# Every operand of the split float32r products at a multiple of 256 bytes in SBUF

## The chip, the core and the metric

The kernel runs on one core of one Trainium2 chip. Its time is the time on the device of one execution, in microseconds (us). The core has a matrix engine (TensorE, PE in the profile; its weight loads are shown apart, as PEld), a vector engine (DVE), an activation engine (ACT), GpSimd (POOL), and queues that start DMA transfers (SP). SBUF is the memory on the chip, 128 partitions wide; an address below is the place of a tile inside each partition, in bytes.

## What is computed

A trunk of two layers on 512 tokens of 1,024 features, all in float32:

```python
for l in range(DEPTH):                       # 2
    h = rms_norm(x, ffn1_norm[l])
    x = x + 0.5 * swiglu_ffn(h, ffn1_w_gate[l], ffn1_w_up[l], ffn1_w_down[l])
    h = rms_norm(x, mix_norm[l])
    (a_q, ..., c_g) = jnp.split(h @ w_in[l], SPLIT_IDX, axis=-1)
    o_a, o_b, o_c = hgrn2_mixer(...), gated_deltanet_mixer(...), retention_mixer(...)
    x = x + jnp.concatenate([o_a, o_b, o_c], -1) @ w_out[l]
    h = rms_norm(x, ffn2_norm[l])
    x = x + 0.5 * swiglu_ffn(h, ffn2_w_gate[l], ffn2_w_up[l], ffn2_w_down[l])
return rms_norm(x, final_norm)
```

`swiglu_ffn` is `(silu(h @ wg) * (h @ wu)) @ wd` with 2,816 hidden features. The three mixers are recurrences over the tokens, worked out in chunks.

## The kernel before, in words

**Split products.** A float32 product of the dense layers is made of float32r products, which run in one pass. Both factors are split: a weight `w` into `hi` (w rounded to float32r, by ACT) and `lo` (w less hi, by DVE or POOL), the activations likewise into `xh`/`xl` (line 379, `split_x`), `ah`/`al` (the gated activations) or `mh`/`ml` (the mixers' outputs). The sum takes three products, hi·hi, hi·lo and lo·hi, for each 128 rows of the contraction; `mm3` (line 202) issues them, line 208 in the profile. A product has a stationary operand of 128 x 128 (in the two-part FFN and the "fm" parts this is a block of the weights) and a moving operand of up to 512 columns (the activations). In the "tm" parts of the mixers it is the other way round: activations stationary, 256 columns of weights moving.

**Weights.** A unit is 128 columns of weights for up to 1,024 rows, 128 x 8 x 128 numbers. `load` (line 183) fetches two units with one DMA into `raw`; `split` (line 194) makes `hi` and `lo` of one unit, in pools of W_BUFS = 4 slots each. One kind of unit, with 264 columns, needs 1,056 numbers, and so every slot is 4,224 bytes long.

**The FFN** (`ffn`) goes through its hidden features in three groups of 8, 8 and 6 units. In a group, `pg` (gate) and `pu` (up) sums alternate, 24 products each; then come the `pd` (down) sums over the group's units, 24 or 18 products each. The last FFN's last `pd` sums run by halves of the tokens, 256 columns at a time (`end`).

**The mixers** (`mix`, `interleave`). The dense products (`ps_fm`, `ps_tm`, `ps_out`, line 251) fill the time in which the chains of the three mixers wait; the order is written out when the program is built, from a rough count of time, and the scheduler that builds the program then moves instructions of an engine within it.

**Where the operands lie.** Pools follow one another in SBUF in the order in which they are opened (from line 1416). In the built program the constants end such that all `xh`/`xl` tiles begin 32 bytes past a multiple of 256. The `hi` and `lo` slots begin alternately 32 and 160 bytes past one, since 4,224 is 16.5 times 256; as gate and up units alternate, every gate unit sits in a slot at 32 and every up unit in one at 160. The pool `m` of 50 tiles of 2,048 bytes, which holds `ah`, `al`, `mh`, `ml`, comes last; its tiles begin 96 bytes past a multiple of 256. The constant matrices `ident` and `tri`, used by transposes and by a few float32 products such as `ps_gr`, begin 128 bytes past one.

**A constant of the mixers.** `b_blocks` starts an inverse from 16 x 16 unit matrices: line 655 copies them from the constants (`eye16`, 256 columns of the constant table) to `blk_x` on POOL.

Of the kernel before, what the change touches and what calls it, by code (L numbers as in the profile page):

```python
# [45 lines left out]
# 2*pi in parts of 12 bits, so that products with integers below 2**12 are exact  # L46
# [12 lines left out]
def constants():  # L59
# [5 lines left out]
    # inside blocks of 32 tokens  # L65
# [6 lines left out]
    parts["eye16"] = np.broadcast_to(np.eye(16).reshape(1, 256), (P, 256))  # L72
# [23 lines left out]
W_BUFS = 4  # L96
STEP = 1600
# [7 lines left out]
# units of the mixers' weights whose lower parts Pool works out  # L105
POOL_LO = range(2, 70, 2)
GROUP = {"a": 0, "b0": 1, "b1": 2, "c": 3}
# the output projection takes the groups of heads in these parts
OUT_PARTS = (('b0', 'c'), ('b1',), ('a',))
PLAN = 't0 b0 a0 ai cq b1 ck bz0 cg a1 ag bz1'  # L110
# chains of each kind that run at once, and all that hold a PSUM bank
# [5 lines left out]
class Engine:  # L117
    """an engine whose instructions are timed roughly, for the order in which the chains' steps are put down."""
# [5 lines left out]
    def __getattr__(self, name):  # L124
        f = getattr(self.engine, name)

        def call(*args, **kw):
# [10 lines left out]
            # functions that need a table keep their order, so that tables change as seldom as planned  # L138
# [22 lines left out]
class Kern:  # L161
# [12 lines left out]
    def t2(self, name, dtype=F32):  # L174
        """512 numbers on each partition, from the pool that all such tiles share."""
        return self.m.tile([P, T], dtype, tag="m", name=name)
# [17 lines left out]
    def split(self, src, shape):  # L194
        hi = self.whi.tile(shape, F32R, tag="hi", name="hi")
        lo = self.wlo.tile(shape, F32R, tag="lo", name="lo")
        self.nc.scalar.copy(hi, src)
        self.count += 1
        (self.nc.gpsimd if self.count in POOL_LO else self.nc.vector).tensor_tensor(lo, src, hi.bitcast(F32), ALU.subtract)
        return hi, lo  # L200

# [9 lines left out]
    def dense_units(self, src, nk, narrow=0, begin=0):  # L211
        """weights in units of 128 columns, loaded 256 at a time but for the first few."""
# [8 lines left out]
    def stream_units(self, plan, w_out):  # L221
        """loads and splits of the weights of a plan and of the output projection, unit by unit."""
# [26 lines left out]
    def mmr(self, ps, a, b, start, stop):  # L249
        """a float32r product; counts the tensor engine's time."""  # L250
        self.nc.tensor.matmul(ps, a, b, start=start, stop=stop)  # L251
        self.spend(np.prod(b.shape[1:]) * 0.42)

    def mmf(self, ps, a, b, start=True, stop=True):
        """a float32 product; counts the tensor engine's time."""
# [13 lines left out]
    def dense_stream(self, plan):  # L269
        """(x*w) @ w_in, a matrix product at a time; each part goes to its callback, not yet scaled by rstd.  # L270
        "fm": 128 features on partitions; "tm": 128 tokens on partitions."""
        for kind, cols, done in plan:
# [16 lines left out]
            else:  # L289
                n = sum(w for _, w in cols)  # L290
                # two token blocks that share a bank are one accumulation group
# [28 lines left out]
        # the output projection but for its last part  # L320
# [17 lines left out]
    def out_rows(self, part):  # L338
        """row blocks of a part of the output projection; how many blocks of columns a unit of its weights has."""
        return [2 * GROUP[g] + i for g in part for i in range(2)], 4 // len(part)  # L340

    def out_part(self, ps, w, i, j, k, start, stop):
        """128 rows of the output projection's sum."""
# [5 lines left out]
    def room(self, n):  # L349
        """leaves n banks for the next dense products: parts that wait to be taken up are, if need be."""  # L350
# [8 lines left out]
    def prepare(self, d, w):  # L359
        """x[d] is final for this stage: its part of the mean square, and the split x*w."""  # L360
# [26 lines left out]
    def rsqrt(self, out, v, shape):  # L387
        """out = v ** -0.5 for a small positive tile: a guess from the exponent, then Newton steps."""
# [30 lines left out]
    def gated(self, pg, pu):  # L419
        """silu(gate) * up, split."""  # L420
# [17 lines left out]
    def ffn(self, wg, wu, wd, layer, norm, meanwhile=None, begun=None):  # L438
        nc = self.nc
        xs = list(self.xs)  # L440
        for gi, (f0, nf) in enumerate(GROUPS):
            act, queue = [], deque()
            gu, uu = self.gate_up(wg, wu, gi) if gi or not begun else begun
            # the first sums wait for the factors of the rows
# [31 lines left out]
    def end(self, units, act, nf):  # L476
        """the last sums and the final norm, by halves of the tokens: the first half leaves while the second is summed.
        x * weight goes to tokens on partitions, then come the row factors."""
# [23 lines left out]
    def to_rows(self, y, i, g):  # L502
        """half of the features of a half of the tokens, tokens on partitions."""
# [31 lines left out]
    def b_gates(self, l, ba):  # L535
        """beta, and the cumulative log decay of each 128 tokens, tokens on partitions."""
# [32 lines left out]
        # the same with heads on partitions, split: rows 0.. and 32.. add up to it  # L569
# [4 lines left out]
    def b_conv(self, l, ps, ch, kind):  # L574
        nc = self.nc
        raw = self.mb.tile([P, CONV_K - 1 + T], F32, tag="braw", name="braw", bufs=2)
# [13 lines left out]
    def b_start(self, l, heads):  # L590
        """silu and l2 norms (over the features, tokens on partitions) for a pair of heads."""
# [14 lines left out]
        # sums over the features, each on the partition of its token  # L606
# [15 lines left out]
    def to_tok(self, src):  # L622
        """blocks of 128 columns, each transposed."""
# [5 lines left out]
    def b_blocks(self, heads):  # L629
        """for a pair of heads the inverses of the diagonal blocks of 16, row by row with a block to a partition;  # L630
        32 x 32 transposes lead there and back."""
# [3 lines left out]
        # [(q b r), k, (head, chunk, b)] -> [(q, head, chunk, b), k, r]  # L635
# [15 lines left out]
        # row k of X: e_k - sum over r < k of N[k, r] X[r]; X as [m, k], twice in the end  # L651
# [3 lines left out]
        nc.gpsimd.tensor_copy(x1, self.c("eye16").rearrange("p (m k) -> p m k", k=16))  # L655
# [22 lines left out]
    def b_chain(self, l, h, q, k, v, k_tm, rq):  # L678
        """gated delta rule of one head in chunks of 128; yields where a result is waited for."""
# [21 lines left out]
        # decays: exp of differences of the cumulative log decay  # L701
# [16 lines left out]
        # attn^T and (N beta)^T  # L718
# [9 lines left out]
        # X = (I + N beta)^-1: blocks of 16 first, then by doubling: X <- X - X C X  # L728
# [5 lines left out]
        # blocks of 32: one to as many partitions  # L734
# [53 lines left out]
        # chunks in order; the products of one share a bank  # L788
# [32 lines left out]
    def open(self, group):  # L821
        """room for the outputs of a group of heads: 256 columns, tokens on partitions, two blocks to a tile."""
# [3 lines left out]
    def head_done(self, group):  # L826
        """the group goes on to norm and gate when its heads and its gate are there."""
# [4 lines left out]
    def out_group(self, group):  # L832
        """head norms and gates of 256 columns; then the same with features on partitions, split in two."""
# [27 lines left out]
    def a_chain(self, l, heads):  # L861
        """HGRN2 for a pair of heads: (z, q) each; yields where a result is waited for."""
# [17 lines left out]
        # log f over [1e-20, 1] within the range of Ln: the part below 2**-40 apart  # L880
        odd = lambda t: t.rearrange("p (n r) -> p n r", r=2)[:, :, 1]
        los = {}
        for h, (z, q) in heads.items():
# [3 lines left out]
            # odd tokens: q * f and k / f  # L887
# [14 lines left out]
    def a_head(self, l, h, b, q, k):  # L902
# [5 lines left out]
        # attention inside 64 tokens, level by level: the later half of each 2s tokens sees the earlier half;  # L908
        # up to 32 tokens in blocks of 32, one to as many partitions
# [5 lines left out]
        # q and k of odd tokens have the step to them within, so that both of a pair share the even one's decay  # L915
# [29 lines left out]
        # all levels up to 64 tokens share a bank  # L945
# [17 lines left out]
        # pairs of tokens  # L963
# [15 lines left out]
        # decays from the start and to the end of each 64  # L979
# [29 lines left out]
        # what the chunks before each 128 hold: rows of the second 64 pass the first one's total, columns alike  # L1009
# [33 lines left out]
    def rope_tables(self):  # L1043
        """cos and sin of positions * frequencies, tokens on partitions."""
# [468 lines left out]
```

## Time and profile before

| what | value |
|---|---|
| median of 3 runs (lowest to highest) | 2222.67 us (2220.6 to 2222.72) |
| span of the profiled execution | 2224.8 us |
| PE busy | 2190.6 us, 98% |
| PEld busy | 1838.3 us, 83% |
| DVE busy | 1143.8 us, 51% |
| ACT busy | 841.2 us, 38% |
| POOL busy | 497.2 us, 22% |
| DMA, share of 16 engines | 29.0% for the kernel's own queue |

The profiled execution is one more execution than the three runs; its span is what the profile gives for its time, and it is 2.1 us above their median. Matrix products overlap in the pipeline: a product's duration in the profile (about 0.39 us for 512 columns) holds its way through the array, and the pace is the step from one product's start to the next one's.

### The profile page before, as it was taken

Reading aid. Unit: us, or ns where it says so; the run is one execution under the profiler, and the core shown is the slowest. Engines: PE = TensorE matmul, PEld = TensorE weight load, DVE = VectorE, ACT = ScalarE, POOL = GpSimd, SP = SyncE. Lnnn points to the kernel's source line nnn. Section 1 sums busy time; section 2 is a strip of 40 time slices with the busy share of each in tenths; the row PEclk is TensorE's granted clock in tenths of the full one; section 3 lists DMA queues with packets and bytes.
Section 4 is the critical chain, followed back from the end, with each engine's and each line's share of the span. In section 5 each row is a group of like instructions: output and inputs, shape, how many; then the busy total and the mean of one; then the engine's idle time right before and its main releaser. Section 6 shows DMA issues by size and latency. Waiting matters only on the chain.

```text
span 2224.8 us, 31771 instructions
## 1 busy us (share of the span) xinstructions
PE 2190.6 (98%) x13079; PEld 1838.3 (83%) x13079; DVE 1143.8 (51%) x1980; ACT 841.2 (38%) x1319; POOL 497.2 (22%) x462
## 2 busy tenths in 40 slices
PE   9999999998999999999999999999999999999998
PEld 7888888887988788888888888888889888888888
DVE  5444335468487743433543343354766876333335
ACT  4322223555455422222332222244654544222225
POOL 2101012454333210101211010133633412101011
PEclk9999999999999999999999999999999999999999
DMA  5323234221113223232332323242211232323223
GB/s 153 127 76 114 76 104 138 71 76 40 58 58 105 94 96 95 76 114 76 95 112 97 95 95 95 81 130 75 77 51 37 77 105 80 110 84 106 86 94 124
DMA packets 197758, 203.21 MB, mean 91 GB/s; under 512 B 7627, under 2 KB 189293, under 8 KB 197613
## 3 DMA queue, kind: packets, MB, share of 16 engines
q1 hardware_dynamic: 197612, 201.18, 29.0%
q8 instruction: 103, 1.69, 0.3%
q14 instruction: 43, 0.34, 0.0%
HBM read 194.87 MB, written 6.29 MB: 90 GB/s over the span
## 4 chain that ended last, share of the span: by engine, by line
PE 87%; DVE 8%; ACT 2%; issue 1%; POOL 0%; DMA 0%; SPq 0%; DVEq 0%; ACTq 0%; POOLq 0%
PE pu L208 22%; PE pd L208 22%; PE pg L208 21%; PE ps_fm L251 8%; PE ps_tm L251 5%; PE ps_out L251 2%; DVE aw L144 1%; PE ps_scan L256 1%; DVE lo L144 1%; PE ps_ss L256 1%; DVE x L144 1%; DVE flo L144 1%; PE ps_ao L256 1%; DVE af L144 1%; ACT hi L144 1%
## 5 line engine op out<-in xcount | busy, mean ns | idle before, releaser
L144 ACT CAST hi<-raw 128x1024 fp32r<-128x1024 f32 (+2 forms) x369 | 377.6, 1024 | 1135.3 <-PE pd L208 325.9
L144 DVE TENSOR_TENSOR lo<-raw,hi 128x1024 fp32r<-128x1024 f32 (+2 forms) x325 | 390.0, 1200 | 79.7 <-ACT hi L144 61.9
L144 POOL TENSOR_TENSOR g<-g,rstd 128x512 f32<-128x512 f32 x88 | 149.7, 1701 | 1152.9 <-ACT g L141 1152.9
L208 PE MATMUL pd<-ah,lo 128*128 128x512 f32 (+1 forms) x752 | 284.8, 379 | 0.0
L208 PE MATMUL pd<-al,hi 128*128 128x512 f32 (+1 forms) x752 | 284.3, 379 | 0.0
L208 PE MATMUL pd<-ah,hi 128*128 128x512 f32 (+1 forms) x752 | 284.2, 378 | 0.0
L208 PE MATMUL pu<-xh,hi 128*128 128x512 f32 x704 | 279.0, 396 | 0.1
L208 PE MATMUL pu<-xh,lo 128*128 128x512 f32 x704 | 278.2, 395 | 0.0
L208 PE MATMUL pu<-xl,hi 128*128 128x512 f32 x704 | 277.8, 395 | 0.0
L208 PE MATMUL pg<-xl,hi 128*128 128x512 f32 x704 | 275.7, 392 | 0.6 <-DVE xl L144 0.6
L208 PE MATMUL pg<-xh,lo 128*128 128x512 f32 x704 | 275.4, 391 | 0.0
L208 PE MATMUL pg<-xh,hi 128*128 128x512 f32 x704 | 275.1, 391 | 0.1
L144 DVE TENSOR_TENSOR u<-pu,g 128x512 f32<-128x512 f32 x88 | 60.9, 692 | 292.6 <-PE pu L208 277.1
L144 DVE SCALAR_TENSOR_TENSOR x<-pd,x 128x512 f32<-128x512 f32 (+1 forms) x104 | 67.4, 649 | 239.5 <-PE pd L208 239.5
L144 DVE TENSOR_TENSOR g<-pg,rstd 128x512 f32<-128x512 f32 x88 | 60.8, 691 | 209.7 <-PE pg L208 209.2
L208 PEld LDWEIGHTS pd<-al,hi 128*128 128x128 f32 x752 | 141.2, 188 | 29.4
L208 PEld LDWEIGHTS pd<-ah,hi 128*128 128x128 f32 x752 | 141.1, 188 | 28.9
L208 PEld LDWEIGHTS pd<-ah,lo 128*128 128x128 f32 x752 | 141.2, 188 | 28.3
L208 PEld LDWEIGHTS pu<-xh,lo 128*128 128x128 f32 x704 | 132.6, 188 | 31.3
L208 PEld LDWEIGHTS pu<-xl,hi 128*128 128x128 f32 x704 | 132.9, 189 | 30.7
L208 PEld LDWEIGHTS pu<-xh,hi 128*128 128x128 f32 x704 | 132.6, 188 | 30.8 <-ACT hi L144 0.5
L208 PEld LDWEIGHTS pg<-xl,hi 128*128 128x128 f32 x704 | 132.4, 188 | 30.2 <-DVE xl L144 1.8
(331 smaller groups left out, 3791.4 us busy)
## 6 DMA issues: line engine op xcount, KB each, us to landing
raw<-in_ffn_w_gate_dram SPq DMA_DIRECT2D x43, 1024.0 KB, 5.3
raw<-in_ffn_w_up_dram SPq DMA_DIRECT2D x43, 1024.0 KB, 5.4
raw<-in_ffn_w_down_dram SPq DMA_DIRECT2D x32, 1024.0 KB, 5.0
raw<-in_w_in_dram SPq DMA_DIRECT2D x20, 1024.0 KB, 5.4
raw<-in_w_in_dram SPq DMA_DIRECT2D x32, 512.0 KB, 3.8
raw<-in_ffn_w_down_dram SPq DMA_DIRECT2D x20, 768.0 KB, 4.4
xd<-x SPq DMA_DIRECT2D x16, 256.0 KB, 2.2
raw<-in_w_out_dram SPq DMA_DIRECT2D x16, 256.0 KB, 2.7
```

The costliest lines, as they stand in the source:

```text
L144: return f(*args, **kw)
L208: self.nc.tensor.matmul(ps, a[:, k, :], b, start=n == 0, stop=n == 3 * nk - 1)
L251: self.nc.tensor.matmul(ps, a, b, start=start, stop=stop)
L256: self.nc.tensor.matmul(ps, a, b, start=start, stop=stop)
```

## The change

The operands' places are moved; what is multiplied by what stays. Four edits do it:

- a pool `pad` of 56 numbers (224 bytes) after the constants, so that the `xsp` pool begins at a multiple of 256 bytes;
- every weight slot is 1,088 numbers (4,352 bytes, 17 times 256) long, and the unit takes its first part (`unit`);
- the pools `m` and `mb` are opened before `tiny`, and the convolution's `braw` (2,060 bytes) gets a pool of its own at the end, so that nothing of an odd length lies ahead of `m`;
- `eye16` leaves the constant table, which makes room; `blk_x` is set by two memsets.

```diff
-    parts["eye16"] = np.broadcast_to(np.eye(16).reshape(1, 256), (P, 256))
...
+UNIT = 1088
+PAD = 56
...
     def split(self, src, shape):
-        hi = self.whi.tile(shape, F32R, tag="hi", name="hi")
-        lo = self.wlo.tile(shape, F32R, tag="lo", name="lo")
+        hi, lo = (self.unit(p, tag, shape) for p, tag in ((self.whi, "hi"), (self.wlo, "lo")))
...
+    def unit(self, pool, tag, shape):
+
+        t = pool.tile([P, UNIT], F32R, tag=tag, name=tag)
+        return t[:, 0:shape[1] * shape[2]].rearrange("p (k f) -> p k f", k=shape[1])
...
-        raw = self.mb.tile([P, CONV_K - 1 + T], F32, tag="braw", name="braw", bufs=2)
+        raw = self.conv.tile([P, CONV_K - 1 + T], F32, tag="braw", name="braw")
...
-        nc.gpsimd.tensor_copy(x1, self.c("eye16").rearrange("p (m k) -> p m k", k=16))
+        nc.gpsimd.memset(x1, 0.0)
+        nc.gpsimd.memset(x[:, 0:496:33], 1.0)
...
             self.const = pool("const", 1)
+            self.pad = pool("pad", 1)
+            self.pad.tile([P, PAD], F32, name="pad")
             self.xsp = pool("xsp", 1)
             self.wraw = pool("wraw", 2)
             self.whi = pool("whi", W_BUFS)
             self.wlo = pool("wlo", W_BUFS)
             self.tmp = pool("tmp", 1)
+            self.m = pool("m", M_BUFS)
+            self.mb = pool("mb", 1)
             self.tiny = pool("tiny", 2)
+            self.conv = pool("conv", 2)
             self.pa = pool("pa", 3, space=PSUM)
             self.pb = pool("pb", 5, space=PSUM)
-            self.mb = pool("mb", 1)
-            self.m = pool("m", M_BUFS)
```

In the built program of the change, all stationary operands of the split products and all their moving operands begin at a multiple of 256 bytes, but for 144 of the 192 products with 264 columns, whose rows of 1,056 bytes begin 32, 64 or 96 past one. `ident` and `tri` stay at 128. The order on PE in the FFNs is the same in both programs. In the mixers the new memsets make the scheduler move a few instructions by a place or some; two places show what that is like.

On POOL, at the start of the first pair's inverse (`blk_x` is the tile of the inverses, `ctmp` a tile of the rotations), before and now:

```order
L144 TENSOR_TENSOR lo<-raw,hi 128x1024
L144 COPY blk_x<-cst 128x16x16
L144 TENSOR_TENSOR ctmp<-craw,sin 128x256
L144 MEMSET aat 128x512
L144 TENSOR_TENSOR ae<-flo 128x128
```

```order
L147 TENSOR_TENSOR lo<-raw,hi 128x1024
L147 MEMSET blk_x 128x16x16
L147 MEMSET blk_x 128x16
L147 TENSOR_TENSOR ctmp<-craw,sin 128x256
L147 MEMSET aat 128x512
L147 TENSOR_TENSOR ae<-flo 128x128
```

One instruction has become two, at the same place.

On PE, in the first layer's mixers, where a chain's 32 small products (`ps_al`) stand among the dense products of a "fm" part (`ps_fm`), before and now:

```order
L251 MATMUL ps_fm<-xl_2477,hi 128x512
L251 MATMUL ps_fm<-xh_2476,lo 128x512
L251 MATMUL ps_fm<-xh_2509,hi 128x512
L256 MATMUL ps_al<-aq,ak 32x32 x32
L251 MATMUL ps_fm<-xl_2510,hi 128x512
```

```order
L258 MATMUL ps_fm<-xl_2484,hi 128x512
L258 MATMUL ps_fm<-xh_2483,lo 128x512
L263 MATMUL ps_al<-aq,ak 32x32 x32
L258 MATMUL ps_fm<-xh_2516,hi 128x512
L258 MATMUL ps_fm<-xl_2517,hi 128x512
```

The chain's products stand one dense product earlier; the products are the same ones.

## Rows read from the trace of the kernel before

**Rows 1.** The page, busy time, share of the span and instructions of PE.
```profile
PE 2190.6 (98%) x13079; PEld 1838.3 (83%) x13079; DVE 1143.8 (51%) x1980; ACT 841.2 (38%) x1319; POOL 497.2 (22%) x462
```
**Rows 2.** The page, chain that ended last, shares of the span by engine.
```profile
PE 87%; DVE 8%; ACT 2%; issue 1%; POOL 0%; DMA 0%; SPq 0%; DVEq 0%; ACTq 0%; POOLq 0%
```
**Rows 3.** The chain in order of time, first FFN: start us, us, engine, tile, products.
```profile
160.55 5.46 PE pg L208 x24
166.01 5.59 PE pu L208 x24
...
237.88 44.51 PE pd L208 x192
```
**Rows 4.** Groups of PE by form: tile<-operands, shapes, count, busy us, mean ns.
```profile
L208 PE MATMUL pu<-xh,hi 128*128 128x512 f32 x704 | 279.0, 396 | 0.1
...
L208 PE MATMUL pg<-xh,hi 128*128 128x512 f32 x704 | 275.1, 391 | 0.1
...
L208 PE MATMUL pd<-ah,hi 128*128 128x512 f32 x656 | 258.0, 393 | 0.0
...
L251 PE MATMUL ps_fm<-xh,hi 128*128 128x512 f32 x320 | 131.1, 410 | 1.7 <-issue 1.7
...
L251 PE MATMUL ps_tm<-hi,xh 128*128 128x256 f32 x448 | 129.5, 289 | 0.0
...
L251 PE MATMUL ps_out<-mh,hi 128*128 128x512 f32 x128 | 50.8, 402 | 1.0 <-DVE x L144 0.5 <-ACT mh L144 0.4
...
L208 PE MATMUL pd<-ah,hi 128*128 128x256 f32 x96 | 26.3, 277 | 0.0
```
**Rows 5.** Timeline of PE in an up unit: start us, duration us, product.
```profile
190.96 0.40 PE L208 MATMUL pu<-xl,hi 128*128 128x512 f32 x1
191.19 0.40 PE L208 MATMUL pu<-xh,lo 128*128 128x512 f32 x1
191.44 0.40 PE L208 MATMUL pu<-xh,hi 128*128 128x512 f32 x1
```
**Rows 6.** Timeline of PE from 446.61 us, first and last of six products.
```profile
446.61 0.63 PE L251 MATMUL ps_fm<-xl,hi 128*128 128x512 f32 x1
...
448.75 0.63 PE L251 MATMUL ps_fm<-xh,hi 128*128 128x512 f32 x1
```
**Rows 7.** The stretch around it: busy us (count) by engine, granted clock, DMA share, GB/s.
```profile
444.50:451.00 6.50, 6.50 (x21) 5.44 (x21) 2.27 (x13) 0.00 (x0) 0.72 (x1) 0.50 0.32 81
```
**Rows 8.** Timeline of PE at `ps_gr`: its first two products, then all eight.
```profile
403.86 0.41 PE L256 MATMUL ps_gr<-cst,g 128*36 128x128 f32 x2
...
403.86 1.06 PE L256 MATMUL ps_gr<-cst,g 128*36 128x128 f32 x8
```
**Rows 9.** Timeline of PE, 256-column products: first and last of 13, then of 23.
```profile
462.29 0.28 PE L251 MATMUL ps_tm<-hi,xh 128*128 128x256 f32 x1
...
463.73 0.28 PE L251 MATMUL ps_tm<-hi,xh 128*128 128x256 f32 x1
...
2205.12 0.28 PE L208 MATMUL pd<-ah,lo 128*128 128x256 f32 x1
...
2207.63 0.28 PE L208 MATMUL pd<-ah,hi 128*128 128x256 f32 x1
```
**Rows 10.** The first mixer stage: PE, PEld, DVE, ACT, POOL busy, clock, DMA share, GB/s.
```profile
385.00:740.00 355.00, 344.10 (x3171) 303.08 (x3171) 237.31 (x566) 183.34 (x351) 135.70 (x160) 0.97 0.23 69
```
**Rows 11.** The page, groups of ACT and DVE that split the weights.
```profile
L144 ACT CAST hi<-raw 128x1024 fp32r<-128x1024 f32 (+2 forms) x369 | 377.6, 1024 | 1135.3 <-PE pd L208 325.9
L144 DVE TENSOR_TENSOR lo<-raw,hi 128x1024 fp32r<-128x1024 f32 (+2 forms) x325 | 390.0, 1200 | 79.7 <-ACT hi L144 61.9
```
**Rows 12.** The page, DMA issues of gate weights: count, KB each, us to landing.
```profile
raw<-in_ffn_w_gate_dram SPq DMA_DIRECT2D x43, 1024.0 KB, 5.3
```
**Rows 13.** Groups of POOL: the copy of `blk_x`, and memsets.
```profile
L144 POOL MEMSET aat<- 128x512 f32 x8 | 4.2, 520 | 0.0
...
L144 POOL COPY blk_x<-cst 128x256 f32<-128x256 f32 x4 | 1.6, 398 | 0.0
```

More of the change, by code (lines that the diff above doesn't have):

```diff
@@ L1448, in run @@
                         raw = self.wraw.tile([P, KD, P], F32, tag="raw", name="raw")
-                        hi = self.whi.tile([P, KD, P], F32R, tag="hi", name="hi")
-                        lo = self.wlo.tile([P, KD, P], F32R, tag="lo", name="lo")
+                        hi, lo = (self.unit(p, tag, [P, KD, P]) for p, tag in ((self.whi, "hi"), (self.wlo, "lo")))
                     for k in range(4 * g, 4 * g + 4, FIRST):
```

## The prediction

> **What bounds the kernel now.** I read the page first: PE is busy for 98% of the span [rows 1], and 87% of the chain that ended last is PE work [rows 2]. So the time is the number of products times their pace, plus what the mixer stages lose. The pace is in the chain in order of time: a gate unit of 24 products takes 5.46 us, which is 227.5 ns each; an up unit 5.59 us, 232.9 ns each; 192 down products 44.51 us, 231.8 ns each [rows 3]. The reader is to see that gate and up differ by 5.4 ns, though both have the same moving operands, the same shapes and the same three combinations. Only the places of their weights (32 or 160 bytes past a multiple of 256) and their banks differ. The groups by form say it again, 391 against 396 ns [rows 4]. Inside an up unit the steps are not even: two neighbours start 0.23 us and then 0.25 us apart [rows 5].
>
> Next I looked for the floor. In a stretch where the granted clock was 0.50 [rows 7], that is 1.2 of 2.4 GHz, six 512-column products with the same kind of operands start 2.14 us apart over five steps, 428 ns each [rows 6]; 512 columns at 1.2 GHz are 426.7 ns. There, nothing but the array's clock sets the pace. Half of it, 213.3 ns, is the floor at the full clock. Gate, up and down products stand 14.2, 19.6 and 18.5 ns above it. So at the full clock something else than the array is too slow, by 6 to 9%, and it depends on where the weights lie: I read it as the supply of the operands from SBUF.
>
> Is there a product at the full clock whose moving operand lies better? `ps_gr` moves `tri`, which begins at 128. Two of its rows take 0.41 us and all eight 1.06 us [rows 8]: the last six steps are 0.65 us, 108 ns each. A row of these float32 products goes through its 128 columns twice, so it should be compared with 256 columns: floor 106.7 ns. Split products with 256 columns and operands at 32, 96 or 160 need 120 ns (12 steps, 1.44 us) in a "tm" part and 114 ns (22 steps, 2.51 us) at the end [rows 9]. So `ps_gr` runs within 2 ns of the floor, the others 7 and 13 above it. The place of the moving operand is one difference; the other is that `ps_gr` loads 36 columns of weights and not 128, so this is a sign and no proof.
>
> **The change part by part.** *The places.* I take it that aligned operands run at or near the floor. The ends of that case: not under 213.3 ns [rows 6]; and not over two steps of `ps_gr`, 218 ns [rows 8]. I take 216, the middle. Then, by counts [rows 4]:
>
> - gate, 3 x 704 = 2112 products: 11.5 ns x 2112 = 24.3 us;
> - up, 2112: 16.9 x 2112 = 35.7 us;
> - down with 512 columns, 3 x 656 = 1968: 15.8 x 1968 = 31.1 us;
> - down with 256 columns, 288: from 114 to 108 ns, 1.7 us.
>
> That is 93 us in the four FFNs, all of it on the path, for PE is never without work there. What could be late next? A unit of weights would be needed every 24 x 216 ns = 5.2 us; ACT rounds one in 1.02 us, DVE takes 1.20 us for its lower part [rows 11], and the 1 MB for two units lands in 5.3 us of the 10.4 us for which two units last [rows 12]. None comes near.
>
> *The mixers.* They hold 3 x 320 + 3 x 128 = 1344 split products of 512 columns ("fm" and the output projection) and 3 x 448 = 1344 of 256 columns [rows 4]. At the mean of gate and up, 230.2 ns, the first give 14.2 x 1344 = 19.1 us; the second, from 120 to 108 ns, give 16.1 us: 35 us. But in the first mixer stage PE is idle for 11 of 355 us and the clock falls at times [rows 10], and the 8% of the chain on DVE [rows 2], some 180 us, lie mostly here. Where a chain's step on DVE or ACT ends a wait, a faster dense product only makes PE wait longer. Nothing before shows the share; the ends are none and all, and I take half, 17 us. What is late there next is DVE, with the chains' steps.
>
> *The rest.* The POOL copy of 398 ns becomes two memsets, four times; a memset of 512 columns took 520 ns [rows 13], so the pair costs 0 to 0.4 us more or less each time, on an engine with 22% of the span [rows 1], beside a chain that waits for DVE at that place. Together below 1 us either way, taken as nothing. If that cover were gone it would be 1.6 us in all. The reordered instructions in the mixers (a chain's `ps_al` ahead of one dense product, and some like it) change when a chain starts by one product, 0.2 us; taken as nothing, and inside the half that I left open. The pad, the longer slots and 256 fewer constant columns add no instruction. No wait and no DMA is added.
>
> The sum: 93 + 17 = 110 us. From the profiled execution, 2224.8 - 110 = 2114.8 us; its span is 2.1 us above the median of the runs, so for the runs 2222.7 - 110 = **2112.7, say 2113 us**. The case's own range: at 213.3 ns and with all of the mixers' part, 107.8 + 2.1 + 40.6 = 150 us, 2072; at 218 ns and with none, 78.7 + 1.4 = 80 us, 2143.
>
> **Rivals.** *Only the unevenness goes.* The starts would matter only against each other (both at 32: 227.5 ns; 32 and 160: 232.9), and what is left over the floor, 14 ns, would be the price of a 4-byte operand or of changing weights under way. Then all products run as the gate's do: 5.4 x 2112 + 4.3 x 1968 = 19.9 us, and half of 2.7 x 1344 = 1.8 us more: 22 us, **2201** (2196 to 2207). For it speaks that nothing before runs 512 columns under 227 ns; against it, `ps_gr`.
>
> *Nothing changes.* What differs between gate and up would not be the place: a bank, or the order of the loads. Then 2222.7, **2223**. For it: the rest of the change moves no work. Against it: the steps inside an up unit differ though they share a bank [rows 5]. The Trainium skill, page "SBUF — State Buffer", section "Door 1: The DMA port swizzle", says that SBUF is read in lines of 16 bytes, and that only crossing into a new line costs; every operand before begins at a multiple of 32 bytes, so by this rule there would be nothing to gain. By the rule, gate and up would run alike; the rows give 227.5 and 232.9 ns, so the trace does not bear it out alone, and I leave this case the chance that the rows leave.
>
> *Slower.* If a weight load and the moving read of the same moment hinder each other when they fall on the same part of a 256-byte stretch, then starts that are all alike bring them together every time. The price is that of the slowest steps seen, some 0.24 us [rows 5], for all: 12.5 x 2112 + 7.1 x 2112 + 8.2 x 1968 = 57.5 us in the FFNs, half of 9.8 x 1344 = 6.6 us in the mixers: 64 us, **2287**. It decides as soon as the mean step goes over 231 ns. Against it: gate products, whose starts are alike already (both at 32), are the fastest ones.
>
> *The change doesn't do what it says.* For 144 products with 264 columns it does not; at a gain of 12 ns each that is 2 us at most, and no case of its own.
>
> **How the numbers follow.** Chances: operands at the floor 0.64, only the unevenness 0.16, nothing 0.12, slower 0.08. A measurement of this kernel can tell 0.2%, 4.4 us, from no change. The first two cases are faster by more: 0.80; same 0.12; slower 0.08. The forecast is that of the likeliest case, 2113, its own range 2072 to 2143. The range for 8 in 10 takes in that case but for its outermost low end, where every term is at its best, and the second case: 2080 to 2207.
>
> **What would show it.** Right: in the chain in order of time, a gate unit and an up unit both take 24 x 216 ns = 5.2 us, 192 down products 41.5 us; 512-column products at the granted clock 0.50 stay at 427 ns; the "tm" products step by 108 ns; PE idles more in the mixer stages. Wrong: gate units that stay at 5.46 us while up units come down to it (the second case); units of 5.6 us or more (the last). If the FFNs gain their 93 us and the total far less, the mixers gave nothing or the scheduler's new order cost something there.

## The result, and the profile after

The change makes the kernel a little faster: 2196.86 us (median of 4 runs, 2189.34 to 2199.5) against 2222.69 us for the kernel before (4 runs, 2220.6 to 2223.48). The ratio is 0.9877, with a 95% interval of 0.986 to 0.9895. All ratios here are of fast executions; one slow execution of the kernel before (2529.8 us, beside `noslots`) is left out. The forecast, 2113 us, was 84 us too low; the rival "only the unevenness goes" had given 2201 us.

The profiled execution after the change has a span of 2197.7 us, 27.1 us less than the one before. The page, busy time of the engines and then the chain that ended last by engine, as in [rows 1, 2]:

```profile
PE 2164.1 (98%) x13079; PEld 1836.0 (84%) x13079; DVE 1147.4 (52%) x1980; ACT 842.8 (38%) x1319; POOL 498.6 (23%) x466
...
PE 89%; DVE 8%; ACT 1%; issue 1%; POOL 0%; DMA 0%; SPq 0%; DVEq 0%; ACTq 0%; POOLq 0%
```

PE is still busy for 98% of the span, and the 8% of the chain on DVE have stayed. What bounds the kernel is the same; PE's 26.5 us less is nearly the whole gain. The chain in order of time (start, us, engine, tile, products), as in [rows 3]:

```profile
158.73 5.44 PE pg L215 x24
164.17 5.44 PE pu L215 x24
...
234.89 43.52 PE pd L215 x192
```

Gate and up units now take the same 5.44 us, or 226.7 ns a product, and the down products take 43.52 us / 192 = 226.7 ns. Before, the three stood at 227.5, 232.9 and 231.8 ns. The 227.5 of a gate unit were not one pace. On the timeline of PE in the kernel before (start us, duration us), the fourth and the 23rd of a unit's 24 products:

```profile
161.08 0.39 PE L208 MATMUL pg<-xh,hi 128*128 128x512 f32 x1
...
165.39 0.39 PE L208 MATMUL pg<-xl,hi 128*128 128x512 f32 x1
```

The 19 steps between them take 4.31 us, 226.8 ns each, the pace after the change; the other five of the unit's 5.46 us, at its two edges next to the up units, take 230 ns each. So a gate product with both operands 32 bytes past a multiple of 256 already ran at 226.7 ns before the change. The groups of PE by form (busy us, mean ns), as in [rows 4]:

```profile
L215 PE MATMUL pg<-xh,hi 128*128 128x512 f32 x704 | 274.5, 390 | 0.2 <-ACT xh L147 0.2
L215 PE MATMUL pu<-xh,hi 128*128 128x512 f32 x704 | 274.4, 390 | 0.0
...
L215 PE MATMUL pd<-ah,hi 128*128 128x512 f32 x656 | 255.3, 389 | 0.0
...
L258 PE MATMUL ps_tm<-hi,xh 128*128 128x256 f32 x448 | 129.6, 289 | 0.0
...
L215 PE MATMUL pd<-ah,hi 128*128 128x256 f32 x96 | 26.9, 284 | 0.0
```

Gate and up have become alike here too (390 against 390 ns, where 391 against 396 stood before). The "tm" products with 256 columns have not moved (289 ns), and the down products with 256 columns got longer, 284 after 277 ns. The timeline of PE in an up unit (start us, duration us), as in [rows 5]:

```profile
186.45 0.39 PE L215 MATMUL pu<-xh,hi 128*128 128x512 f32 x1
186.68 0.39 PE L215 MATMUL pu<-xl,hi 128*128 128x512 f32 x1
186.90 0.39 PE L215 MATMUL pu<-xh,lo 128*128 128x512 f32 x1
```

The steps are 0.23 and 0.22 us: even, where 0.23 and 0.25 stood in the rows before. So the unevenness went, and the price above the floor of 213.3 ns stayed. Two more places on the timeline tell what kind of price it is. First a stretch at the half clock (granted clock 0.52, window and then the first and last of eight products), as in [rows 6, 7]:

```profile
440.00:445.00 5.00, 5.00 (x14) 3.89 (x14) 2.27 (x13) 0.00 (x0) 0.00 (x0) 0.52 0.37 104
```

```profile
440.86 0.63 PE L258 MATMUL ps_fm<-xh,lo 128*128 128x512 f32 x1
...
443.85 0.63 PE L258 MATMUL ps_fm<-xh,hi 128*128 128x512 f32 x1
...
2178.08 0.28 PE L215 MATMUL pd<-ah,hi 128*128 128x256 f32 x1
...
2180.96 0.28 PE L215 MATMUL pd<-ah,hi 128*128 128x256 f32 x1
```

Seven steps take 2.99 us, 427 ns each: at 1.2 GHz nothing has changed and nothing is over the floor. The last two rows are the first and last of 25 down products with 256 columns, at the full clock: 24 steps take 2.88 us, 120.0 ns each. The difference between 512 and 256 columns is 226.7 - 120.0 = 106.7 ns, which is just 256 columns at 2.4 GHz. So with equal starts a product of the FFNs pays 13.3 ns over its columns, whether it has 256 of them or 512. With equal starts it is a price per product and no slower rate.

**Where the 27.1 us came from.** By counts and the chain's rows: gate (5.46 - 5.44) / 24 x 2112 = 1.8 us; up (5.59 - 5.44) / 24 x 2112 = 13.2 us; down (44.51 - 43.52) / 192 x 1968 = 10.1 us; the 288 down products with 256 columns, from 114 to 120 ns, cost 1.7 us. That is 23.4 us in the FFNs. The first mixer stage runs from the first "tm" product to the first gate product of the next FFN: on the timeline of PE from 376.17 to 738.46 us after the change, from 381.92 to 747.47 us before. That is 362.3 us after 365.6, a gain of 3.3 us; the second stage gained 1.6 us in the same way. Cut at the same places, the FFNs' stretches gained 5.8, 12.7 and 3.7 us, 22.2 together, and with 4.9 in the mixers that is the 27.1 us seen. The counts give 1.2 us more for the FFNs; the rounding of a unit's time to 0.01 us alone is worth about 0.9 us on each of the first two terms.

### The profile page after: what moved, and what is told of

Its sections match the earlier page's. It is cut to its first block, busy times and chain, and to the rows that moved or that the text cites. A ratio compares the mean times of both kernels' runs of the same rounds, so it can differ in the third digit from the quotient of the medians.

```text
span 2197.7 us, 31776 instructions
## 1 busy us (share of the span) xinstructions
PE 2164.1 (98%) x13079; PEld 1836.0 (84%) x13079; DVE 1147.4 (52%) x1980; ACT 842.8 (38%) x1319; POOL 498.6 (23%) x466
## 4 chain that ended last, share of the span: by engine, by line
PE 89%; DVE 8%; ACT 1%; issue 1%; POOL 0%; DMA 0%; SPq 0%; DVEq 0%; ACTq 0%; POOLq 0%
PE pd L215 22%; PE pu L215 22%; PE pg L215 21%; PE ps_fm L258 8%; PE ps_tm L258 6%; PE ps_out L258 2%; PE ps_scan L263 1%; DVE aw L147 1%; DVE lo L147 1%; DVE x L147 1%; PE ps_ss L263 1%; PE ps_ao L263 1%; DVE xl L147 1%; PE ps_al L263 0%; PE ps_y L263 0%
## 5 line engine op out<-in xcount | busy, mean ns | idle before, releaser
L215 PE MATMUL pu<-xh,hi 128*128 128x512 f32 x704 | 274.4, 390 | 0.0
L147 DVE SCALAR_TENSOR_TENSOR x<-pd,x 128x512 f32<-128x512 f32 (+1 forms) x104 | 67.4, 649 | 230.8 <-PE pd L215 230.5
L215 PEld LDWEIGHTS pg<-xh,hi 128*128 128x128 f32 x704 | 132.3, 188 | 27.9 <-ACT xh L147 0.4
```

The lines of the kernel that those rows point to most:

```text
L147: return f(*args, **kw)
L215: self.nc.tensor.matmul(ps, a[:, k, :], b, start=n == 0, stop=n == 3 * nk - 1)
```

## The experiments

The theory after the result: **the distance counts.** What the change took away is a hindrance between a weight load and a moving read that depends on where the two start against each other. What the runs can show is that dependence; that it is a weight load that hinders the read is inferred. Against it stand the theory of **alignment** (a multiple of 256 is itself what helps), the edit's other parts, and the question of what the remaining 13.3 ns are. All kernels are the changed one with the edit shown, unless the text says otherwise.

**1. Everything 32 bytes past a multiple (`all32`).** All operands keep their distances, and none is aligned any longer.

```diff
-PAD = 56
+PAD = 64
```

> The pad is 32 bytes longer, so every operand of the split products begins 32 bytes past a multiple of 256: the places relative to each other stay as in the change, none is aligned. Theory 'distance' (what costs is the distance between the start of the weights and the start of the moving operand, and the change makes it 0 everywhere): gate, up and down products all step by 226.7 ns, time 2197 us (2190 to 2203). Theory 'alignment' (an operand that begins off a 256-byte boundary costs more): back towards the pace of before, over 2210 us.

Measured: 2195.29 us (2190.27 to 2196.53), ratio to the kernel before 0.9877 (0.9862 to 0.9893): the whole gain, without alignment. The chain in order of time:

```profile
158.49 5.44 PE pg L215 x24
163.93 5.44 PE pu L215 x24
...
234.65 43.52 PE pd L215 x192
```

Row for row the same times as with everything at multiples of 256. Alignment itself does nothing.

**2. The longer slots alone (`slots`).** The kernel before, with slots of 1,088 numbers; no pad, no other order of pools. The constants make room as in the change. Weights and `xh`/`xl` are then all at 32, the down products' activations at 96, a distance of 192.

```diff
+UNIT = 1088
...
-        hi = self.whi.tile(shape, F32R, tag="hi", name="hi")
-        lo = self.wlo.tile(shape, F32R, tag="lo", name="lo")
+        hi, lo = (self.unit(p, tag, shape) for p, tag in ((self.whi, "hi"), (self.wlo, "lo")))
```

> The kernel before with the longer weight slots alone (and the constant left out, for room): x tiles and all weight slots at 32, the m tiles still at 96. Theory 'distance': gate and up both at 226.7 ns (up was 232.9), down with 512 columns at 230.5 as its half with slots at 32 before, 256-column down products at 113.7: 12.9 + 2 + 2.5 us less in the FFNs and 2 in the mixers, about 2203 us (2198 to 2209). Theory 'alignment': nothing is aligned, so 2222 us, or some part of the gain only if 32 happens to be better than 160.

Measured: 2197.47 us (2193.86 to 2199.19), ratio 0.9894 (0.9877 to 0.991). The chain:

```profile
158.45 5.44 PE pg L211 x24
163.89 5.44 PE pu L211 x24
...
234.61 43.96 PE pd L211 x192
```

Gate and up are at the floor of the change; down products at a distance of 192 take 229.0 ns, not the 230.5 that I had expected, and the time is just under the expected 2198 to 2209. One of the four edits, with the constant that makes room for it, brings nearly all that the change brings.

**3. All but the longer slots (`noslots`).** `UNIT = 1088` becomes 1056 again; pad, order of pools and memsets stay. The slots lie alternately at 0 and 128.

> The change without the longer weight slots: moving operands at 0, weight slots alternately at 0 and 128, so that gate units are at distance 0 and up units at 128 again, and down units half and half. Theory 'distance': gate 226.7 ns, up 232.4 as when all weights stood at 128, down 229.5 on the mean: 5.7 x 2112 + 2.8 x 1968 = 17.5 us more than the change in the FFNs and 2 to 4 in the mixers, about 2216 us (2211 to 2221). Theory 'alignment to 128 bytes': 2197.

Measured: 2213.7 us (10 runs, 2211.8 to 2219.94) against 2223.35 us (12 runs) for the kernel before beside it, ratio 0.9968 (0.9956 to 0.998). The chain:

```profile
159.44 5.46 PE pg L215 x24
164.91 5.59 PE pu L215 x24
...
236.77 44.16 PE pd L215 x192
```

Gate and up are as before the change, though the pad has put their activations at a multiple of 256. The down products, half of whose weights now start level with `ah`/`al`, take 230.0 ns: about the middle between 226.7 (level) and 232.4 (128 apart, next run). The distance decides unit by unit, and the pad, the order of the pools and the memsets, all still in, bring little.

**4. All weights 128 bytes on (`w128`).** All operands at multiples of 128, every pair 128 apart.

```diff
-        return t[:, 0:shape[1] * shape[2]].rearrange("p (k f) -> p k f", k=shape[1])
+        return t[:, 32:32 + shape[1] * shape[2]].rearrange("p (k f) -> p k f", k=shape[1])
```

> The change with all weights 128 bytes further on in their slots: moving operands at 0, weights at 128 (the reverse in the 256-column products of the mixers). Theory 'distance': every 512-column product runs as the up products did, 232.5 ns: 5.9 ns x 6192 = 36 us more in the FFNs and some 4 in the mixers, about 2237 us (2228 to 2246), slower than before. Theory 'alignment' with a boundary of 128 bytes or less: 2197 us.

Measured: 2233.22 us (2231.66 to 2234.49), ratio 1.0052 (1.0037 to 1.0067): slower than the kernel before, by a move of 128 bytes. The chain:

```profile
161.19 5.58 PE pg L215 x24
166.77 5.57 PE pu L215 x24
...
239.27 44.62 PE pd L215 x192
```

The gate, which nothing had been able to slow so far, takes 232.4 ns like the rest. With 1 and 4 the matter of the gain is settled for products with 512 columns: what counts is the distance of the starts.

The 288 down products with 256 columns go the other way. They step by 114 ns before the change [rows 9], by 118 in `slots`, by 119 in `noslots` and `w128`, and by 120 with equal starts, in the change and in `all32`. In `slots` the first and last of 21 (20 steps, 2.35 us):

```profile
2147.32 0.28 PE L211 MATMUL pd<-ah,hi 128*128 128x256 f32 x1
...
2149.67 0.28 PE L211 MATMUL pd<-ah,lo 128*128 128x256 f32 x1
```

Equal starts are the slowest place for them among these six kernels. Before the change they step alike with weights at 32 and at 160, and with all weights at 32 in `slots` they step by 4 ns more, with activations at 96 in both. So the distance modulo 256 does not tell all of their pace.

**5 and 6. Which distances (`sweep16`, `sweep4`).** In the FFNs, successive pairs of units start 0, 16, ... 240 bytes into their slots (`sweep16`), or 0, 4, ... 60 bytes (`sweep4`, without the last `* 4`).

```diff
+        o = 0
+        if self.count >= 1000 and shape[1] * shape[2] <= 1024:
+            self.slot = getattr(self, "slot", 0) + 1
+            o = (self.slot - 1) // 4 % 16 * 4
+        return t[:, o:o + shape[1] * shape[2]].rearrange("p (k f) -> p k f", k=shape[1])
```

> The change, with the FFNs' weights placed 0, 16, 32, ... 240 bytes into their slots in turn (gate and up unit of a pair alike), moving operands at 0: one run gives the step of 512-column products by distance. Theory 'two reads of the same memory' (weights and moving operand are read at once and now and then want the same part): 226.7 ns at 0, 232.4 at 128 as when all stood there, values between and around them elsewhere, by 16-byte steps in no simple order; mean about 231, the time about 2220 us. Theory 'each on its own' (no place of one matters beside the other): 226.7 throughout, 2196 us. Open in either: whether some distance runs below 226.7.

> The same in steps of 4 bytes, 0 to 60. Theory 'two reads of the same memory': if the parts are as wide as 64 bytes or more, steps change little and evenly over this range, from 226.7 at 0 to some 228 to 231 near 60; if they are narrow, 16 bytes or less, the step jumps at their edges. Theory 'each on its own': 226.7 throughout, 2196 us.

The chain of `sweep16`, gate units at 224, 240, 0 and 32 bytes:

```profile
172.34 5.60 PE pg L219 x24
...
183.54 5.46 PE pg L219 x24
...
194.44 5.44 PE pg L219 x24
...
216.21 5.59 PE pg L219 x24
```

And of `sweep4`, gate units at 0, 4 and 8 bytes:

```profile
195.08 5.45 PE pg L219 x24
...
205.98 5.58 PE pg L219 x24
...
217.14 5.54 PE pg L219 x24
```

The mean steps over all units at a distance, in ns:

| distance, bytes | `sweep16` | `sweep4` |
|---|---|---|
| 0 | 227.1 | 227.2 |
| 4, 8, 12 | | 232.4, 230.7, 230.4 |
| 16 | 227.3 | 233.4 |
| 20 to 60 | (32, 48: 232 to 234) | 230 to 235 |
| 176, 192 | 229.9, 229.0 | |
| 240 | 227.1 | |
| all others | 232 to 234 | |

For 512 columns level starts are the best place (at 0 a unit's own pace is 226.7; its border with a unit at another distance makes the rest), and a single number beside them (4 bytes) already costs 5 ns. Multiples of 256 are as good as 0 (all distances of the change are such), while 64 and 128 are not, so the good place comes back every 256 bytes and not more often. It isn't the whole law: 16 bytes give 227.3 in one sweep and 233.4 in the other, where the same distance falls on other slots. Whatever else in the addresses matters there is open. `sweep4` took 2222.83 us in one run. `sweep16` took 4220.36 us, and that time can't be compared: from some 1.78 ms on its granted clock was 0.16, as the last section shows. Its steps above are from before that.

**7. Fewer weight columns (`short`).** What are the 13.3 ns that are left? If the weights' read takes turns with the moving one, a shorter weight load should cost less. Up products load 32 columns, down products 64, but for the first and last of a sum.

```diff
+                c = P if n in (0, 3 * nk - 1) else cols
-                self.nc.tensor.matmul(ps, a[:, k, :], b, start=n == 0, stop=n == 3 * nk - 1)
+                self.nc.tensor.matmul(ps[0:c], a[:, k, 0:c], b, start=n == 0, stop=n == 3 * nk - 1)
```

> The change, but between the first and the last product of each sum the up products take only 32 of their 128 weight columns, the down products (but for the last ones by halves) 64. It leaves out most of the terms of the other columns. What are the 10.8 ns by which a 512-column product with equal starts stays over the 215.8 ns that it took with one activation column repeated? Theory 'two reads': they are lost while weights are read beside the moving operand, and go with the number of weight columns: up some 218.5 ns, down 221. Theory 'moving operand alone': both stay at 226.7. Theory 'fixed price of changing weights': both stay at 226.7 too, and the difference of the two is for the repeated column's run to tell, which speaks against this one already.

Measured, in one run: 2207.83 us. The page and the chain:

```profile
PE 2173.4 (99%) x13079; PEld 1583.2 (72%) x13079; DVE 1143.3 (52%) x1980; ACT 841.5 (38%) x1319; POOL 502.3 (23%) x466
```

```profile
159.35 5.44 PE pg L216 x24
164.79 5.55 PE pu L216 x24
...
236.31 44.12 PE pd L216 x192
```

PEld fell by 253 us, and the products did not get faster but slower: 231.3 ns on the mean of a unit with 32 columns (up), 229.8 with 64 (down), while the untouched gate kept its 226.7. A shorter weight load does not lower the price. Why it raises it is open.

**8. One address again and again (`repeat`).** Up products read one column of weights 128 times, down products one column of activations 512 times.

```diff
+                a_ = a[:, k, :] if same != "w" else a[:, k, 0:1].to_broadcast([P, P])
+                b_ = b if same != "x" else b[:, 0:1].to_broadcast([P, b.shape[1]])
```

> The change, but the up products take one column of weights 128 times, and the down products (but for the last ones by halves) one column of activations 512 times; the gate products stay. It leaves out the true values of up and down. What is the 13.3 ns over 213.3 that every aligned 512-column product still has? If the reading of the weights takes it from the moving operand: up 213 to 216 ns, down 226.7. If the supply of the moving operand alone is too slow: down 213 to 216, up 226.7. If it is a fixed price of changing weights, whatever is read: all three 226.7.

Measured, in one run: 2183.58 us. The chain:

```profile
163.07 5.55 PE pu L217 x24
...
234.54 41.44 PE pd L217 x192
```

Down products come to 41.44 us / 192 = 215.8 ns, 2.5 over the floor: the first split products anywhere in this case that run there. Up products with repeated weights take 231 ns. So 11 of the 13.3 ns hang on how the moving operand is read.

**9. How far the moving read spreads (`foot`).** If the two reads share a memory whose parts follow from the address modulo 256 bytes, a moving operand that stays in a small part should do worse, and one that goes round 256 bytes no worse than a long one. The moving operand goes round 16 columns (64 bytes) in the gate, 64 columns (256 bytes) in up, 256 columns in down.

```diff
+                    b_ = b[:, 0:f].unsqueeze(1).to_broadcast([P, T // f, f])
+                    p_ = ps.rearrange("p (r f) -> p r f", f=f)
```

> The change, with moving operands that go round in a small piece of their tile: gate products over 16 columns (64 bytes) 32 times, up products over 64 columns (256 bytes) 8 times, down products (but for the last by halves) over 256 columns twice. It leaves out the true values of gate, up and down. One column repeated took 215.8 ns, the whole tile takes 226.7. Theory 'price per start': what counts is that two reads begin together, so all three stay near 226.7, or above where the small piece meets the weights more often. Theory 'price per stretch of memory read': 216 for 64 bytes, a little more for 256, near 226.7 for 1024. Theory 'memory cells are shared by address modulo 256 bytes': 64 bytes can meet the weights in one part only and 256 bytes in all, so gate differs clearly from up, and up equals down.

Measured, in one run: 2221.78 us. The chain:

```profile
161.12 5.81 PE pg L219 x24
166.94 5.46 PE pu L219 x24
...
240.04 43.52 PE pd L219 x192
```

The gate takes 242 ns, the worst mean step of all runs; up 227.5, down 226.7 as in the change. In up, the excess lies in the first three products behind a gate unit, and the others step by 226.7. That is as a memory in 256-byte rounds would have it, but does not show one: the moving read also goes round its piece 32 times in the gate, 8 times in up and twice in down, and no run parts the size of the piece from the number of rounds. Nor does the idea explain by itself why `repeat`, whose moving read stays in 4 bytes, has the best step of all.

**10. Weights in steps of 8 bytes (`stride`).** `hi` and `lo` lie interleaved in one tile, so each read of weights goes in steps of 8 bytes while the moving one goes in steps of 4; the units' starts sweep 0 to 244 bytes. If the two reads only had to stay out of step, another distance should take the place of 0.

```diff
+            v = t[:, o:o + 2 * n].rearrange("p (k f r) -> p k f r", k=shape[1], r=2)
+            return v[:, :, :, 0], v[:, :, :, 1]
```

> The change, with hi and lo of an FFN unit interleaved, so that weights are read in steps of 8 bytes and not of 4, and begin 0, 16, ... 240 bytes into their slot in turn. If weights and moving operand are read at once, the moving one twice as fast, a step of 8 bytes makes them advance alike: they should then either meet all the time or never. Theory 'two reads': the step depends strongly on the distance, near 216 ns for some distances and far over 230 for others. Theory 'alignment of each': 226.7 at all distances, or more for the strided read. Theory 'moving operand alone': no step below 226.7. No total is forecast, 2180 to 2300 us.

Measured, in one run: 2239.41 us. Two gate units of the chain, at 0 and at 48 bytes:

```profile
195.21 5.58 PE pg L220 x24
...
228.75 5.54 PE pg L220 x24
```

By distance, the mean steps over all units go from 230.0 to 233.5 ns, with 233.0 at 0; a unit's `lo` begins 4 bytes further than its `hi`, so each mean is of two distances. There is no good place left, and the idea in that form falls. Among these runs, 226.7 ns needed equal starts *and* equal steps.

**11. Another order of the three products (`order`).** If the 13.3 ns were paid for turning to another moving tile, keeping `xh` for two products would save some.

```diff
-            for a, b in ((wh, xh), (wh, xl), (wl, xh)):
+            for a, b in ((wh, xh), (wl, xh), (wh, xl)):
```

> The change with two of the three products of each step exchanged: hi and lo weights follow each other on the same moving operand, so that every third product reads the moving tile that the one before it read. Theory 'price per start' (each product pays a fixed price when its two reads begin, whatever it read before): nothing changes, 226.7 ns, 2196 us (2190 to 2203). Theory 'price of a new moving tile': a third of the steps falls towards 216 ns, 3.6 ns on the mean, some 25 us less, 2171.

Measured: 2194.14 us (2193.29 to 2195.92), ratio 0.9875 (0.9858 to 0.9891). The chain:

```profile
164.24 5.44 PE pu L215 x24
...
234.96 43.52 PE pd L215 x192
```

The step is the same 226.7 ns, and the ratio's interval lies on that of the change. The order doesn't matter.

No run points to a version that beats the change: `all32`, `slots` and `order` are within the scatter of its runs, and `repeat` doesn't compute the trunk.

## Why the prediction was wrong

**What bounds the kernel: right.** PE at 98% of the span before and after, and products times the pace measured after gave the FFNs' gain within 1.2 us.

**The floor: right.** 427 ns at the granted clock 0.52, as before; and `repeat` shows that a split product can come to 215.8 ns at the full clock.

**The step that failed** is the sentence "I take it that aligned operands run at or near the floor". It rested on `ps_gr` [rows 8], whose step I compared with 256 columns because a float32 product goes through its 128 columns twice. It was the wrong yardstick. After the change, with `tri` still at 128, all eight of its rows take 1.06 us as before (timeline):

```profile
398.00 1.06 PE L263 MATMUL ps_gr<-cst,g 128*36 128x128 f32 x8
```

Its pace is still 108 ns a step, while split products with 256 columns and both operands at multiples of 256 step by 120.0. I had named the other difference myself, the 36 columns of weights, and called the row no proof; then I put 0.64 on it. `short` shows that 32 columns of weights don't bring a split product near the floor either (231.3 ns at 512 columns). In place of the floor the runs show 226.7 ns for 512 columns and 120.0 for 256, 13.3 ns over it, aligned or not (`all32`). What lets `ps_gr` run there is open: it is also float32 and not float32r, which no run tests. What the runs show is that neither the alignment nor fewer weight columns does it for split products.

**The terms of the sum.** Gate: 0.8 ns a product instead of 11.5, and that at the edges of its units alone. Up: 6.2 instead of 16.9. Down: 5.2 instead of 15.8. Each is short by about 10.6 ns, the same amount: the 226.7 that is really left less the 216 that I took. The down products with 256 columns, 6 ns faster in the forecast, got 6 ns slower, since for them equal starts are the slowest place seen (120 ns against 114); why, no run tells. The mixers: 4.9 us instead of 17, and not because waits ate it. Here is the first stage, as in [rows 10]:

```profile
381.00:732.00 351.00, 341.09 (x3160) 301.66 (x3159) 238.17 (x566) 184.11 (x352) 136.92 (x161) 0.97 0.23 70
```

PE is idle for 10 of 351 us, where it was idle for 11 of 355. The pace simply gained little there, and the "tm" products stayed at 120 ns.

**The rivals.** "Only the unevenness goes" was right in that the starts matter against each other (`all32`, `w128`), in its size (22 us forecast, 25.8 us between the medians) and its range (2196 to 2207). What it said of the rest over the floor is not shown: 11 of the 13.3 ns hang on the moving read, and whether a 4-byte operand or changing weights has a part in it is open. Its case was in the rows: gate products were level at 32 bytes and took 227.5 ns [rows 3], and no unit with 512 columns was ever under 227. A rival that asks for no step outside what was seen deserved more than 0.16, and the range reached 2207 only because of it.

"Nothing changes" fell with the up units. `w128` speaks directly on the rule that I weighed there, from the Trainium skill, page "SBUF — State Buffer", section "Door 1: The DMA port swizzle" (only a new 16-byte line costs): a shift by 128 bytes, eight such lines, moved the step from 226.7 to 232.4 ns, so the rule does not cover two reads at a time. The Trainium skill's page "TensorE: Matmul & The Clock Gate", section "Step-by-step: what each phase is for", says that TensorE reads weights and moving operand through independent ports, and that loading weights takes nothing from the moving read. By that rule the distance of their starts would not matter; here the measurement decides, and it is worth 5.7 ns a product.

"Slower" had it the wrong way round for 512 columns: equal starts are the best place, not the worst. (For the few down products with 256 columns its sign was right.) A weight start 128 bytes off is what costs, and it costs less than I put on it (2233 us, not 2287).

**The small terms held.** The memsets of `blk_x`, group by tile (count, least/median/most ns):

```profile
L147 POOL MEMSET blk_x<- x8: 126/218/333, 474.8 to 1684.7; 128x256 f32 x4, 128x16 f32 x4
```

A pair takes some 440 ns where the copy took 398 [rows 13], four times: nothing, as taken. And nothing came late next, since the weights' supply never had to go faster than a unit every 5.44 us.

## What to carry to other kernels

When neighbouring products of one kind differ in pace, look at where their two operands start: here levelling the start of the weights with that of the moving operand, modulo 256 bytes, was worth 1.2%, and padding a slot to a multiple of 256 did nearly all of it, because the activations already began at the same 32 bytes. That holds for moving operands of 512 columns; the down products with 256 columns lost 6 ns each by it, so the shape that fills the time has to be measured. To tell a distance from an alignment, shift everything together, and then one operand alone; the two runs cost a number each. And a floor is read from the same kind of product: a float32 product with 36 columns of weights told nothing about float32r products with 128.

## What the runs showed of the hardware

- **The pace depends on where weights and moving operand start against each other.** With 512 columns at the full clock a product steps by 226.7 ns with level starts (modulo 256 bytes), by 229 to 235 at most other distances, and by 242 when the moving operand goes 32 times round 64 bytes. At 1.2 GHz it is 427 ns, before the change, after it and with all weights 128 bytes on (`w128`).
- **With 256 columns the order is another.** Down products step by 120.0 ns with level starts, by 118 to 119 in `slots`, `noslots` and `w128`, and by 114 before the change.
- **With level starts the price is one per product.** 13.3 ns over the columns' own time, for 256 columns and for 512. For 512 columns order, alignment and fewer weight columns don't lower it; reading a single moving column does (2.5 ns). What it consists of is open.
- **Fewer or repeated weight columns cost time.** 32 columns: 231.3 ns; one column read 128 times: 231 ns; 128 columns in a row: 226.7.
- **A granted clock of 0.16, once.** In `sweep16` the granted clock, after 80 us at 1.00 with PE busy for 79 of them, was 0.16 from 1.78 ms to the end of the run, which is neither 1.2 nor 2.4 GHz. The windows (PE, PEld, DVE, ACT, POOL busy, clock, DMA share, GB/s):

```profile
1700.00:1780.00 80.00, 79.08 (x919) 71.89 (x918) 65.78 (x180) 43.79 (x82) 29.71 (x45) 1.00 0.26 79
1800.00:4200.00 2400.00, 2400.00 (x2064) 1735.88 (x2063) 194.06 (x303) 142.97 (x200) 53.78 (x40) 0.16 0.05 17
```

No other run showed it, and nothing here tells its cause.
